# Two of the four sums of weight quarters per feed-forward unit made by accumulating transfers instead of VectorE

## The chip, the cores and the metric

The kernel runs on one core of one Trainium2 chip. The metric is the time that the device takes for one execution, in microseconds (us); comparisons are between medians of several runs.

## What is computed

The reference is two stacks of layers over a sequence of 512 tokens of width 1024. The first stack has two layers, each with a feed-forward block, a mixer (stick-breaking attention beside a gated delta rule), a cross attention to a memory and a second feed-forward block. The second stack has two layers of hybrid attention with a gated residual. All of it is in fp32. The change touches the four feed-forward blocks alone:

```python
def swiglu_ffn(x, w_in, w_out):          # w_in: 1024 x 5632, w_out: 2816 x 1024
    gate, up = jnp.split(x @ w_in, 2, axis=-1)
    return (jax.nn.silu(gate) * up) @ w_out

for l in range(DEPTH):                   # DEPTH = 2
    h = h + 0.5 * swiglu_ffn(rms_norm(h, ffn1_norm[l]), ffn1_w_in[l], ffn1_w_out[l])
    h = h + hybrid_mixer(...)
    h = h + memory_cross_attention(...)
    h = h + 0.5 * swiglu_ffn(rms_norm(h, ffn2_norm[l]), ffn2_w_in[l], ffn2_w_out[l])
```

## The kernel before

TensorE multiplies in a rounded fp32 format. To keep accuracy each operand is split into a rounded part (`hi`, made by ScalarE, line 394) and the rest (`lo`, made by VectorE, line 395), and every product is three matmuls: hi with hi, hi with lo, lo with hi.

A feed-forward block (`ffn`, line 472) has 11 units of 256 hidden columns. Units 0 and 1 are computed plainly (`ffn_plain`). Units 2 to 10 are computed by `ffn_seven_steps` (line 549) with Strassen's scheme in Winograd's form: the input projection of a unit is a 2 x 2 product of blocks, gate and up columns by the two halves of the 1024 inputs, and is made with seven block products instead of eight. The sums of the activations that the scheme needs are made once per block (`seven_parts`, line 522). The sums of the weights are made per unit: with the quarters b11 (gate, first half), b12 (up, first half), b21 (gate, second half) and b22 (up, second half), each 128 x 1024 fp32 or 512 KB, they are p1 = b11 + b12, p2 = p1 + b22, b12 + b22 and p2 + b21. All four are made by VectorE (`tt`, line 562).

The seven products of a unit come in the order b11, p2, b12 + b22, p1, b21, p2 + b21, b22. Ahead of each, `parts` rounds its weights: a ScalarE cast into a tile `sh` and a VectorE subtraction into a tile `sl`, two buffers of each. So the rounding for one product can start when the product two before it has been computed. Below, the "third rounding" of a unit is the pair of cast and `sl` for its third product, and so on. `product` (line 580) issues 24 matmuls of 256 columns. A `yield` behind each product lets `ffn` put one or two steps of the output projection of earlier units between the products (line 274 on TensorE). In unit 2, the first of a block that uses seven products, there are no earlier units whose output projection could run, so its products follow each other directly.

The weight quarters and their sums lie in tiles with the tag `sr`, of which there are six. They are taken in program order and a tile is reused when its last reader is done; a transfer that is to fill one waits for that. In a unit of the kernel before they are taken by b11, b12, p1, b22, p2 and b21.

All weight transfers go through SP's queue in order (`load`, lines 564 to 567 for the quarters; line 266 for the other weights). The code in `with ahead()` is given a priority 110 instructions earlier than its place, so loads, sums and roundings run ahead of the products. The order of the instructions on each engine is made by a scheduler when the program is built; on the chip each engine takes its own in that order and waits on semaphores. POOL (GpSimd) has next to nothing to do in the feed-forward blocks.

Of the kernel before, what the change touches and what calls it, by code (L numbers as in the profile page):

```python
# [14 lines left out]
ALU = mybir.AluOpType  # L15
# [162 lines left out]
class Builder:  # L178
# [370 lines left out]
    def ffn_seven_steps(self, name, l, u, ap, xh, xl, s, R, t, act):  # L549

        nc = self.nc
        toks = slice(0, HS), slice(HS, S)
        A = lambda th, kh: [x[:, 4 * kh : 4 * kh + 4, toks[th]] for x in (xh, xl)]
        ahead = lambda: self.tc.high_priority(offset=FF_AHEAD)
        T = lambda: ap.tile([P, 4, 256], F32, name=self.uid("sr"), tag="sr", bufs=6)
        v = lambda x: x.rearrange("p (j c) -> p j c", j=2)  # L560
        Rh = [R[:, ts].unsqueeze(1).to_broadcast([P, 2, HS]) for ts in toks]
        tt = lambda o, a, b, op=ALU.add: nc.vector.tensor_tensor(out=o, in0=a, in1=b, op=op)

        def load(c, kh):
            w = T()
            nc.sync.dma_start(out=w, in_=self.waps(name + "_in", l, 2 * u + c).rearrange("p (k c) -> p k c", k=8)[:, 4 * kh : 4 * kh + 4])
            return w

        def parts(w):
            x = [ap.tile([P, 4, 256], F32R, name=self.uid(n), tag=n, bufs=2) for n in ("sh", "sl")]  # L570
            self.split(*x, w)
            return x

        def product(ps, w, x, first=True):
            for j in range(2):
                fs = slice(j * P, (j + 1) * P)
                for k in range(4):
                    start = first and j == 0 and k == 0
                    for i, (a, b) in enumerate(((0, 0), (0, 1), (1, 0))):
                        nc.tensor.matmul(ps[:, j], w[a][:, k, fs], x[b][:, k], start=start and i == 0, stop=k == 3 and i == 2, skip_group_check=True)  # L580

        xt = lambda tag: v(self.xp.tile([P, S], F32, name=self.uid(tag), tag=tag, bufs=1))
        a, b, c, d = (self.ps("d", [P, 2, HS]) for _ in range(4))
        with ahead():
            b11 = load(0, 0)
            w = parts(b11)
        product(a, w, A(0, 0))
        m1 = xt("acc")
        nc.scalar.copy(m1, a)
        yield  # L590
        with ahead():
            b12 = load(1, 0)
            p1 = T()
            tt(p1, b11, b12)
            b22 = load(1, 1)
            p2 = T()
            tt(p2, p1, b22)
            w = parts(p2)
        product(b, w, s["s2"])
        V = xt("sq")  # L600
        tt(V, m1, b)
        yield
        with ahead():
            tt(b12, b12, b22)
            w = parts(b12)
        product(c, w, s["s3"])
        x22 = v(t("uu"))
        tt(x22, V, c)
        yield
        with ahead():  # L610
            w = parts(p1)
        product(d, w, s["s1"])
        tt(x22, x22, d)
        tt(x22, x22, Rh[1], ALU.mult)
        yield
        with ahead():
            b21 = load(0, 1)
            w = parts(b21)
        product(a, w, A(0, 1), False)
        gates = v(t("gg")), v(t("gg"))  # L620
        ss = [v(t("ss")) for _ in range(2)]
        tt(gates[0], a, Rh[0], ALU.mult)
        nc.scalar.activation(out=ss[0], in_=gates[0], func=AF.Silu)
        yield
        with ahead():
            tt(p2, p2, b21)
            w = parts(p2)
        product(c, w, A(1, 1), False)
        tt(gates[1], V, c)
        tt(gates[1], gates[1], Rh[1], ALU.mult)  # L630
        nc.scalar.activation(out=ss[1], in_=gates[1], func=AF.Silu)
        yield
        with ahead():
            w = parts(b22)
        product(d, w, s["s4"], False)
        x12 = v(t("uu"))
        tt(x12, V, d)
        tt(x12, x12, Rh[0], ALU.mult)
        for th, x in ((1, x22), (0, x12)):
            nc.vector.scalar_tensor_tensor(out=x, in0=x, scalar=-1.0, in1=ss[th], op0=ALU.mult, op1=ALU.mult)  # L640
            self.split(*(y[:, :, toks[th]] for y in act), x)
        yield
# [1013 lines left out]
```

## Time and profile before

| | us |
|---|---|
| median of 3 runs | 3196.88 |
| lowest and highest run | 3195.92, 3201.14 |
| the profiled execution, its own time | 3195.22 |
| span of the profiled execution, first to last instruction | 3192.9 |
| TensorE busy | 3134.1 |
| VectorE busy | 2326.2 |
| ScalarE busy | 1451.7 |
| POOL busy | 133.8 |

The profile is of one execution. Times in it are counted from the start of its span. Busy times overlap, since the engines work beside each other. TensorE's granted clock is at its full level in the four stretches that the change touches.

### The profile page before, as it was taken

What the parts mean: (1) busy time and instruction counts of PE and PEld (TensorE: products, weight loads), DVE (VectorE), ACT (ScalarE), POOL (GpSimd) and SP (SyncE); (2) the same over time, 40 slices, a digit from 0 to 9 for tenths busy, and PEclk for the clock granted to TensorE, in tenths of its full rate; (3) what the DMA queues carried; (4) which work ended last, traced back from release to release, by engine and by line L of the source; (5) the groups of instructions that cost most, each with busy time, mean ns of one, the idle gap of its engine ahead of it and who ended that gap; (6) DMA issues with size and microseconds to landing.
All of it is one profiled execution on the core that took longest, in us unless ns stands there. A gap on an engine that the chain in (4) does not pass through costs nothing. (4 is left out here: it accounts for less than half of the span.)

```text
span 3192.9 us, 50423 instructions
## 1 busy us (share of the span) xinstructions
PE 3134.1 (98%) x20520; PEld 2718.9 (85%) x20520; DVE 2326.2 (73%) x3952; ACT 1451.7 (45%) x2291; POOL 133.8 (4%) x182
## 2 busy tenths in 40 slices
PE   8999999989999999999999989999999999999999
PEld 7999877778889998999877868889998987799877
DVE  8887567776588877888657686578886667766675
ACT  5344542544443434334452354453343556445563
POOL 0000002220000000000002040000000000000000
PEclk9999999999999999999999999999999999999999
DMA  4332220323233323333221223133332322223223
GB/s 165 97 118 81 87 73 28 95 71 113 67 125 95 107 76 117 100 103 101 70 86 34 82 65 119 60 125 99 101 95 72 100 80 80 76 90 100 72 73 101
DMA packets 86728, 287.32 MB, mean 90 GB/s; under 512 B 10080, under 2 KB 13408, under 8 KB 86496
## 3 DMA queue, kind: packets, MB, share of 16 engines
q1 hardware_dynamic: 86496, 284.10, 28.7%
q8 instruction: 161, 2.64, 0.3%
q14 instruction: 71, 0.58, 0.1%
HBM read 269.38 MB, written 2.10 MB: 85 GB/s over the span
## 5 line engine op out<-in xcount | busy, mean ns | idle before, releaser
L268 DVE TENSOR_TENSOR wl<-wr,wh 128x1024 fp32r<-128x1024 f32 (+3 forms) x384 | 443.1, 1154 | 211.4 <-ACT wh L267 209.4
L267 ACT CAST wh<-wr 128x1024 fp32r<-128x1024 f32 (+3 forms) x384 | 378.1, 985 | 399.4 <-PE psd L274 285.9
L394 ACT CAST sh<-sr 128x1024 fp32r<-128x1024 f32 x252 | 264.8, 1051 | 503.7 <-PE psd L580 474.4
L274 PE MATMUL psd<-xh,wh 128*128 128x512 f32 x960 | 387.0, 403 | 7.2 <-ACT xh L397 7.2
L274 PE MATMUL psd<-xl,wh 128*128 128x512 f32 x960 | 385.5, 402 | 0.2 <-DVE xl L398 0.2
L274 PE MATMUL psd<-xh,wl 128*128 128x512 f32 x960 | 384.9, 401 | 0.2 <-DVE wl L268 0.2
L580 PE MATMUL psd<-xh,sl 128*128 128x256 f32 x1152 | 322.7, 280 | 5.2 <-DVE sl L395 5.2
L580 PE MATMUL psd<-xh,sh 128*128 128x256 f32 x1152 | 322.5, 280 | 0.0
L580 PE MATMUL psd<-xl,sh 128*128 128x256 f32 x1152 | 321.9, 279 | 0.0
L395 DVE TENSOR_TENSOR sl<-sr,sh 128x1024 fp32r<-128x1024 f32 x252 | 307.3, 1220 | 15.1 <-ACT sh L394 14.2
L274 PE MATMUL psd<-wh,xh 128*128 128x256 f32 (+1 forms) x1024 | 292.1, 286 | 1.0 <-ACT wh L267 0.9
L274 PE MATMUL psd<-wh,xl 128*128 128x256 f32 (+1 forms) x1024 | 289.9, 283 | 1.2 <-DVE xl L398 1.1
L274 PE MATMUL psd<-wl,xh 128*128 128x256 f32 (+1 forms) x1024 | 289.0, 283 | 0.0
L274 PE MATMUL psd<-ah,wh 128*128 128x512 f32 x704 | 278.2, 395 | 0.0
L274 PE MATMUL psd<-al,wh 128*128 128x512 f32 x704 | 278.0, 395 | 0.0
L274 PE MATMUL psd<-ah,wl 128*128 128x512 f32 x704 | 277.0, 394 | 0.0
L274 PEld LDWEIGHTS psd<-xh,wh 128*128 128x128 f32 x960 | 181.2, 189 | 53.9 <-ACT xh L397 7.2
L580 PEld LDWEIGHTS psd<-xh,sl 128*128 128x128 f32 x1152 | 216.9, 188 | 6.8 <-DVE sl L395 6.8
L580 PEld LDWEIGHTS psd<-xh,sh 128*128 128x128 f32 x1152 | 216.8, 188 | 5.3
L580 PEld LDWEIGHTS psd<-xl,sh 128*128 128x128 f32 x1152 | 216.8, 188 | 4.8
L274 PEld LDWEIGHTS psd<-xh,wl 128*128 128x128 f32 x960 | 181.5, 189 | 42.1 <-issue 1.2
L274 PEld LDWEIGHTS psd<-xl,wh 128*128 128x128 f32 x960 | 181.5, 189 | 39.9 <-DVE xl L398 1.0
(452 smaller groups left out, 6999.2 us busy)
## 6 DMA issues: line engine op xcount, KB each, us to landing
sr<-w_ffn_in_dram SPq DMA_DIRECT2D x144, 512.0 KB, 3.9
wr<-w_ffn_out_dram SPq DMA_DIRECT2D x96, 384.0 KB, 4.0
wr<-w_ffn_in_dram SPq DMA_DIRECT2D x32, 512.0 KB, 3.8
wr<-w_mix_gdn_dram SPq DMA_DIRECT2D x24, 512.0 KB, 3.7
B<-B SPq DMA_DIRECT2D x40, 256.0 KB, 3.4
wr<-w_ffn_out_dram SPq DMA_DIRECT2D x16, 512.0 KB, 3.4
wr<-w_mix_qk_dram SPq DMA_DIRECT2D x16, 512.0 KB, 3.8
wr<-w_x_k_dram SPq DMA_DIRECT2D x16, 512.0 KB, 3.7
```

Of the source, the lines that this page charges most:

```text
L267: nc.scalar.copy(hi, raw)
L268: (nc.gpsimd if name in ON_POOL else nc.vector).tensor_sub(lo, raw, hi.bitcast(F32))
L274: mm = lambda a, b, first, last: nc.tensor.matmul(ps, a, b, start=first, stop=last, skip_group_check=flip)
L394: nc.scalar.copy(hi, src)
L395: nc.vector.tensor_tensor(out=lo, in0=src, in1=hi.bitcast(F32), op=ALU.subtract)
L580: nc.tensor.matmul(ps[:, j], w[a][:, k, fs], x[b][:, k], start=start and i == 0, stop=k == 3 and i == 2, skip_group_check=True)
```

## The change

A helper `src` names a weight quarter in memory. `load` takes a second quarter, `more`: after the plain transfer on SP's queue a second transfer, issued by POOL, adds that quarter to the same tile while it is written. p1 = b11 + b12 is loaded so (b11 a second time, b12 added), and so is b12 + b22, as b22 a second time with b12 added. The two VectorE sums for these go, and so does the plain load of b12 alone. The `sr` tiles of a unit are then taken by b11, p1, b22, p2, b22 + b12 and b21; b11's tile is no longer read by a sum.

```diff
+        src = lambda c, kh: self.waps(name + "_in", l, 2 * u + c).rearrange("p (k c) -> p k c", k=8)[:, 4 * kh : 4 * kh + 4]
+
-        def load(c, kh):
+        def load(c, kh, more=None):
+
             w = T()
-            nc.sync.dma_start(out=w, in_=self.waps(name + "_in", l, 2 * u + c).rearrange("p (k c) -> p k c", k=8)[:, 4 * kh : 4 * kh + 4])
+            nc.sync.dma_start(out=w, in_=src(c, kh))
+            if more:
+                nc.gpsimd.dma_start(out=w, in_=src(*more), accum_op=ALU.add)
             return w
...
         with ahead():
-            b12 = load(1, 0)
-            p1 = T()
-            tt(p1, b11, b12)
+            p1 = load(0, 0, (1, 0))
             b22 = load(1, 1)
             p2 = T()
             tt(p2, p1, b22)
...
         with ahead():
-            tt(b12, b12, b22)
-            w = parts(b12)
+            w = parts(load(1, 1, (1, 0)))
         product(c, w, s["s3"])
```

## Rows read from the trace of the kernel before

**Rows 1.** The page, busy time of each engine: us, share of the span, instructions.

```profile
PE 3134.1 (98%) x20520; PEld 2718.9 (85%) x20520; DVE 2326.2 (73%) x3952; ACT 1451.7 (45%) x2291; POOL 133.8 (4%) x182
```

**Rows 2.** Stretches with seven-product units: us, busy time by engine (instructions), clock, DMA, GB/s.

```profile
57.40:326.90 269.50, 268.98 (x1905) 251.42 (x1904) 219.89 (x275) 109.53 (x137) 1.25 (x6) 1.00 0.32 100
...
sum 1077.50, PE 1072.32 PEld 1002.47 DVE 867.98 ACT 427.37 POOL 2.51; mean PE 268.08 PEld 250.62 DVE 217.00 ACT 106.84 POOL 0.63
```

**Rows 3.** Waits of TensorE: us in total, times, longest us.

```profile
PE psd L580 <- DVE sl L395: 5.2, 8, 1.8
```

**Rows 4.** Groups by line and shape, VectorE: busy us, mean ns, idle before, releaser.

```profile
L395 DVE TENSOR_TENSOR sl<-sr,sh 128x1024 fp32r<-128x1024 f32 x252 | 307.3, 1220 | 15.1 <-ACT sh L394 14.2
...
L562 DVE TENSOR_TENSOR sr<-sr,sr 128x1024 f32<-128x1024 f32 x144 | 173.4, 1221 | 18.6 <-DMA sr<-w_ffn_in_dram 17.7
```

**Rows 5.** Waits of SP's queue: us in total, times, longest us.

```profile
SPq L566 <- DVE sl L395: 772.8, 120, 8.9
```

**Rows 6.** Stretch from the start to the first seven-product unit, columns as in rows 2.

```profile
0.00:57.40 57.40, 49.77 (x208) 39.46 (x209) 47.25 (x88) 34.21 (x48) 1.53 (x10) 1.00 0.54 182
```

**Rows 7.** DMA issues (KB each, median us to landing) and landing times of `sr` loads.

```profile
sr<-w_ffn_in_dram SPq DMA_DIRECT2D x144, 512.0 KB, 3.9
...
wr<-w_s_ple_dram SPq DMA_DIRECT2D x8, 256.0 KB, 2.6
...
DMA to landing us min/median/max: 3.5/3.9/7.6
```

**Rows 8.** Timeline of a handover beside output steps: start, us, engine, line, what.

```profile
241.73 0.33 SPq L566 DMA_DIRECT2D sr<-w_ffn_in_dram  x1
...
250.06 1.23 DVE L395 TENSOR_TENSOR sl<-sr,sh 128x1024 fp32r<-128x1024 f32 x1 [0.28 <-ACT sh L394]
251.21 0.95 DVE L268 TENSOR_TENSOR wl<-wr,wh 128x768 fp32r<-128x768 f32 x1
252.66 0.69 DVE L562 TENSOR_TENSOR uu<-uu,psd 128x512 f32<-128x512 f32 x1 [0.50 <-PE psd L580]
253.38 0.69 DVE L562 TENSOR_TENSOR uu<-uu,R 128x512 f32<-128x512 f32 x1
253.99 1.22 DVE L395 TENSOR_TENSOR sl<-sr,sh 128x1024 fp32r<-128x1024 f32 x1
255.33 2.36 DVE L562 TENSOR_TENSOR sr<-sr,sr 128x1024 f32<-128x1024 f32 x2
...
258.97 0.28 PE L580 MATMUL psd<-xh,sl 128*128 128x256 f32 x1
...
269.19 1.22 DVE L395 TENSOR_TENSOR sl<-sr,sh 128x1024 fp32r<-128x1024 f32 x1
```

**Rows 9.** Timeline of the first block's first seven-product unit.

```profile
62.62 0.33 SPq L566 DMA_DIRECT2D sr<-w_ffn_in_dram  x1
...
66.44 1.22 DVE L562 TENSOR_TENSOR sr<-sr,sr 128x1024 f32<-128x1024 f32 x1 [0.98 <-DMA sr<-w_ffn_in_dram]
...
69.45 0.39 PE L580 MATMUL psd<-xh,sl 128*128 128x256 f32 x1 [0.21 <-DVE sl L395]
...
70.64 1.22 DVE L395 TENSOR_TENSOR sl<-sr,sh 128x1024 fp32r<-128x1024 f32 x1
...
72.36 0.28 PE L580 MATMUL psd<-xh,sl 128*128 128x256 f32 x1
...
73.21 1.23 DVE L562 TENSOR_TENSOR sr<-sr,sr 128x1024 f32<-128x1024 f32 x1 [0.19 <-DMA sr<-w_ffn_in_dram]
74.36 1.22 DVE L395 TENSOR_TENSOR sl<-sr,sh 128x1024 fp32r<-128x1024 f32 x1
...
75.63 0.39 PE L580 MATMUL psd<-xh,sl 128*128 128x256 f32 x1 [0.30 <-DVE sl L395]
```

**Rows 10.** Timeline of the third block's first seven-product unit.

```profile
1286.02 1.22 DVE L562 TENSOR_TENSOR sr<-sr,sr 128x1024 f32<-128x1024 f32 x1 [0.98 <-DMA sr<-w_ffn_in_dram]
...
1294.33 1.22 DVE L562 TENSOR_TENSOR sr<-sr,sr 128x1024 f32<-128x1024 f32 x1 [1.74 <-DMA sr<-w_ffn_in_dram]
```

## The prediction

> **What bounds the kernel now.** The page's busy times come first: TensorE is busy for 3134.1 of 3192.9 us, VectorE for 2326.2 [rows 1]. The change lies in the four feed-forward blocks, so the next view is the table of stretches over the part of each block in which the seven-product units run (nine units each, 36 in all): of 1077.50 us TensorE is busy for 1072.32, VectorE for 867.98 [rows 2]. The reader is to see two things there. VectorE has about a fifth of its time free; and TensorE stands still for 1077.50 - 1072.32 = 5.2 us in all four stretches together. The view of waits says what for: matmuls of line 580 waited eight times for a `sl` from VectorE, 5.2 us in total, 1.8 at the longest [rows 3]. So whatever VectorE is spared, these stretches can give back 5.2 us at most, 0.16% of the time. VectorE's sums are not on the path that sets the end, but a VectorE that stands waiting can get onto it.
>
> **What the change removes.** Of the 144 sums on line 562, 1.22 us each [rows 4], two per unit go: 72 x 1.22 = 88 us of VectorE. All of it lies beside TensorE's work; on the path it is worth a share of the 5.2 us.
>
> **What it adds.** Per unit one more plain load on SP (five for four) and two accumulating ones issued by POOL, each of which must wait for the plain load that fills its tile. POOL does nothing else in the stretches but a few memsets, so no one queues behind these waits there. On SP the extra issue costs nothing as long as tiles, not SP, set the pace, and they do: 120 loads waited for a `sl`, 772.8 us [rows 5]. The extra traffic is three 512 KB reads per unit, 108 x 0.524 MB = 56.6 MB, in 1077.50 us 53 GB/s on top of about 100 there; the first 57 us moved 182 GB/s [rows 6], so bandwidth covers it.
>
> What counts is the time L from the landing of the plain load to that of the accumulating one, because the sum that VectorE still makes of the two (p2 = p1 + b22) needs it, and VectorE takes its instructions in order. No accumulating transfer is in the trace. A plain 512 KB load lands after a median of 3.9 us, a 256 KB one after 2.6 [rows 7]: that is about 1.3 us fixed and 2.6 per 512 KB. An addition to what is already there has to move the new and the old data: 1.3 + 2 x 2.6, my estimate is **L = 6.4 us**. The lower end is a plain load's 3.9; the upper, three such loads one after another (read, read back, write), 11.7. A gain below 3.9 has no reason, since the source is the same. The Trainium skill, page "DMA: Bandwidth & Descriptors", section on the anatomy of a DMA from GpSimd, gives 2.0 us plus bytes over 436 GB/s for one issued there, 3.2 us for this size by an estimate from it; it is for a plain copy, and no run here shows one from that queue. By it nothing in the sum below would be late, and the first rival's time would hold.
>
> **Where L is covered: a unit beside output steps.** 28 of the 32 handovers between units are of this kind. The six `sr` tiles go round in the order in which they come free. The plain half of p1 takes the tile that the third rounding pair has read, so its load starts where one starts today, at 241.73, and lands 3.9 later at 245.63; with L it is summed at 252.0. p2 takes the tile of b21, free when the fifth `sl` ends (250.06 + 1.22 = 251.28), one rounding earlier than today's 255.33 [rows 8], where all times of this part stand. VectorE waits 0.7 us there in the worst order. Behind the sum stand a `wl`, two evictions and the sixth `sl`: 1.23 + 0.95 + 0.69 + 0.69 + 1.22 = 4.78, which ends at 256.8, and the matmul that reads that `sl` runs at 258.97. Cost nothing, with 2.2 us left. The other new tile, s = b22 + b12, takes the tile freed by the sixth `sl` (255.21): 255.21 + 3.9 + 6.4 = 265.5, and its `sl` is at 269.19, behind its ScalarE cast: covered too, and its VectorE sum is gone from ahead of it.
>
> **Where it is not: the first unit of each block, four times.** There nothing runs between the products, and all eight TensorE waits stand here, two in each block [rows 9]. Today p1's sum for the next unit waits for its load and holds up the fifth `sl`; the p2 sum then stands right ahead of the seventh `sl` [rows 9]. In the changed kernel p1's sum is no longer in VectorE's queue, so the fifth `sl` is on time. The load is issued at 62.62 and had landed by 66.44; with L, 72.84. That is before 73.21, where p2's sum stands now, so if p2's sum stays ahead of the seventh `sl`, that `sl` comes about 0.3 us earlier, in three of the four blocks alike. In the third block p2's sum waited 1.74 us for b22, whose load the new order starts a rounding earlier: 1286.02 + 6.4 = 1292.4 against 1294.33 [rows 10], 1.9 us earlier. **Sum:** 3 x 0.3 + 1.9 = 2.8 us less. The profiled execution took 3195.22, so 3192.4; the median of the three runs is 1.66 above it, so **3194**. This is a change of 0.1%, below the 0.2% that a measurement here can tell from none.
>
> **Rivals.** *All waits go.* If the accumulation takes no longer than a plain load, 3.9, all 5.2 us vanish: 3191.7. For it: VectorE loses 88 us and has no late input left. Against it: the seventh `sl` also follows a p2 sum and a rounding cast, which stay.
>
> *The sum moves ahead.* p2's tile comes free at the fifth `sl`, so the scheduler may put its sum ahead of the sixth `sl` in the first unit, where it stands behind it today. VectorE then waits until 72.84, and sum and `sl` end 2 x 1.22 later, at 75.28; the matmul that needs this `sl` was at 72.36 [rows 9], 72.0 without the wait that is gone. That is 3.3 us in each of four blocks, 13.2 - 5.2 = 8.0 more: 3204.9, slower by 0.25%. For it: p1's sum stands right behind the `sl` that freed its tile today. Against it: an order by when data come would put the sixth `sl` first.
>
> *The accumulation is long.* In units beside output steps the path is touched once 241.73 + 3.9 + L + 4.78 passes 258.97, that is from **L = 8.6** on; each microsecond more then costs up to 28 us, for VectorE waits in order and everything behind p2's sum is late. At 11.7 it is 3.1 x 28 = 87 there and 4 x 5.3 - 2.8 = 18 in the first units, some 3302. For it: plain loads already took up to 7.6 us to land [rows 7], and these come on top of more traffic. What could stretch them is POOL, which has to issue them, held up by a VectorE that is busy four fifths of the time. The Trainium skill, page "SBUF — State Buffer", box on VectorE blocking a DMA, says that a transfer issued from GpSimd starves while VectorE runs a copy in a two-port mode, 620 ns becoming 3100. By that, L would grow by 2.5 us to 8.9 and the time by some 16 us. The same page says that a tensor_tensor has no such mode, and the VectorE groups of rows 4 are all tensor_tensor; so the trace gives this rule little hold here.
>
> **How the numbers follow.** The forecast (L from about 4 to 8, p2's sum behind the sixth `sl`) has 0.55, all waits gone 0.16, the sum ahead 0.14, long accumulations 0.15. Faster by over 0.2% means below 3190.5, which even the whole 5.2 us does not reach; it takes that and a lucky order elsewhere, or scatter: 0.07 from the first rival, 0.03 from the forecast. Slower by over 0.2% means above 3203.3: 0.15 from long accumulations, 0.12 from the sum ahead. The rest, 0.63, is no difference. The range goes from 3190 (3191.7 less the 1.0 by which the lowest run lay under the median, rounded out) to 3220: the sum ahead lies within it, and so do long accumulations up to L = 9.0, where (9.0 - 8.6) x 28 + 4 x 2.6 - 2.8 = 19 us are added to 3196.9, and the highest run lay 4 above the median. Only longer accumulations are left out above.
>
> **What would show it.** Right: VectorE's busy time lower by some 88 us, 72 sums left on line 562, TensorE's idle time in the four stretches still a few us, with waits for `sl` in the first units alone. L is read from the accumulating transfers' landing times. The sum ahead shows as one wait of some 3 us per block before a sixth product; long accumulations as `sr` sums on VectorE waiting for DMA by several us in most units, and TensorE waiting for `sl` in them. The prediction is wrong if TensorE's idle time grows in units beside output steps, if ScalarE's cast of s waits for its transfer, or if time moves outside these four stretches, of which the sum says nothing.

## The result and the profile after

| | before | after |
|---|---|---|
| median, us | 3197.95 (4 runs, 3195.92 to 3201.14) | 3227.98 (4 runs, 3225.65 to 3232.56) |
| span of the profiled execution, us | 3192.9 | 3224.8 |
| ratio, 95% interval | | 1.0096, 1.0084 to 1.0109 |

The changed kernel is slower by 0.96%. That is outside the predicted range, which ended at 3220.

First the page of the changed kernel: busy time by engine, the two DMA queues (packets, MB, share of 16 engines' span), and the issues of `sr` tiles.

```profile
PE 3141.7 (97%) x20520; PEld 2726.4 (85%) x20520; DVE 2238.0 (69%) x3880; ACT 1452.2 (45%) x2291; POOL 196.2 (6%) x254
...
q1 hardware_dynamic: 91680, 302.97, 30.6%
q0 software_dynamic: 10368, 37.75, 6.6%
...
sr<-w_ffn_in_dram SPq DMA_DIRECT2D x180, 512.0 KB, 4.5
...
sr<-w_ffn_in_dram POOLq DMA_DIRECT2D x72, 512.0 KB, 7.6
```

The change does what it says: VectorE is busy for 88.2 us less than in [rows 1]. The accumulating transfers take a median of 7.6 us from issue to landing, and the plain ones have gone from 3.9 [rows 7] to 4.5. TensorE is busy for longer, 3141.7 against 3134.1, with the same 20520 matmuls.

The table of the four stretches (columns as in [rows 2]), its first row and the sum:

```profile
57.17:340.97 283.80, 273.87 (x1905) 255.95 (x1904) 200.31 (x259) 109.22 (x136) 14.90 (x22) 0.98 0.52 138
...
sum 1107.14, PE 1082.41 PEld 1012.48 DVE 788.59 ACT 427.00 POOL 57.63; mean PE 270.60 PEld 253.12 DVE 197.15 ACT 106.75 POOL 14.41
```

Of the 31.9 us that the span grew by, 1107.14 - 1077.50 = 29.6 lie here. TensorE's idle time has gone from 5.2 to 1107.14 - 1082.41 = 24.7, that is 19.5 more; the other 10.1 are busy time, the same matmuls at a lower clock. The waits of TensorE (us in total, times, longest) name the places:

```profile
PE psd L585 <- DVE sl L395: 19.2, 5, 5.4
PE psd L274 <- ACT xh L397: 8.3, 1, 8.3
PE psn L428 <- DVE acc L419: 5.5, 1, 5.5
...
PE psn L405 <- DVE rc L388: 2.7, 2, 1.4
```

The second row lies ahead of the first block's units and was 7.2 us before; the others are new or longer.

**The first unit of each block** (here and below, the first that uses seven products). Measured from the first matmul of a unit to that of the next, these took 26.6, 27.4, 26.0 and 26.6 us against 20.9, 22.4, 22.5 and 21.0: 19.8 more. The timeline of the one in the first block (it answers to [rows 9]):

```profile
66.59 0.85 POOL L571 DMA_DIRECT2D sr<-w_ffn_in_dram  x1 [27.31 <-DMA sr<-w_ffn_in_dram]
...
73.84 1.23 DVE L562 TENSOR_TENSOR sr<-sr,sr 128x1024 f32<-128x1024 f32 x1 [4.35 <-DMA sr<-w_ffn_in_dram]
74.98 1.22 DVE L395 TENSOR_TENSOR sl<-sr,sh 128x1024 fp32r<-128x1024 f32 x1
...
76.26 0.58 PE L585 MATMUL psd<-xh,sl 128*128 128x256 f32 x1 [4.42 <-DVE sl L395]
```

The sum on VectorE is p2's. It stands ahead of the sixth `sl` and holds VectorE for 4.35 us until the accumulation has landed; TensorE then stands for that `sl`. The matmul at 76.26 takes 0.58 us, twice the usual 0.28. The windows of the same stretch say why:

```profile
72.00:74.00 2.00, 0.00 (x0) 0.00 (x0) 0.16 (x1) 0.56 (x1) 0.00 (x0) 0.98 0.22 43
74.00:76.00 2.00, 0.00 (x0) 0.00 (x0) 2.00 (x2) 0.00 (x0) 0.00 (x0) 0.50 0.00 0
76.00:80.00 4.00, 3.74 (x17) 3.75 (x18) 2.53 (x4) 0.63 (x1) 0.00 (x0) 0.50 0.46 154
80.00:84.00 4.00, 4.00 (x33) 4.00 (x32) 2.80 (x4) 1.78 (x3) 0.86 (x1) 0.90 0.61 136
```

TensorE did nothing between 72 and 76, the granted clock fell from 1.00 to 0.50 (1.2 of 2.4 GHz) and stayed there until past 80, so the products behind the wait ran at half speed for over 4 us. The Trainium skill, page "TensorE: Matmul & The Clock Gate", Part 1, says that the low clock is the default and that activity lifts it; the rows agree.

**Unit 6 of the first block**, 41.3 us against 32.6. Here the memory of the cross attention is read in eight 128 KB loads (`memT`), squared by ScalarE and summed by VectorE, and matmuls of line 428 sum the result. From the timeline, with the rows of SP, POOL, ScalarE and TensorE:

```profile
187.82 0.33 SPq L569 DMA_DIRECT2D sr<-w_ffn_in_dram  x1
...
188.72 0.85 POOL L571 DMA_DIRECT2D sr<-w_ffn_in_dram  x1 [15.10 <-DMA sr<-w_ffn_in_dram]
...
189.00 7.93 SPq L1099 DMA_DIRECT2D memT<-memT_dram  x3
...
196.16 0.42 ACT L418 ACTIVATE sq<-memT 128x256 f32<-128x256 f32 x1 [3.79 <-DMA memT<-memT_dram]
...
200.90 0.80 PE L428 MATMUL psn<-consts,acc 128*128 128x1 f32 x3 [5.50 <-DVE acc L419]
```

A small load issued at 189.0, right behind a plain 512 KB load and an accumulating one, was read only at 196.16. The landing times of these eight loads in the changed kernel, and below them in the kernel before:

```profile
DMA to landing us min/median/max: 2.4/3.1/7.1
```

```profile
DMA to landing us min/median/max: 2.4/2.4/2.9
```

TensorE stood for 5.5 us and then ran at half clock, as the window behind it shows:

```profile
201.00:206.00 5.00, 5.00 (x20) 4.61 (x21) 3.87 (x13) 1.43 (x2) 0.86 (x1) 0.50 0.32 105
```

**The heads of the second and third block** lost 1.4 us each. In the second, p2's sum for the first seven-product unit stands within a chain of small VectorE steps (lines 386 to 388) at whose end TensorE waits:

```profile
914.32 1.23 DVE L562 TENSOR_TENSOR sr<-sr,sr 128x1024 f32<-128x1024 f32 x1 [1.41 <-DMA sr<-w_ffn_in_dram]
...
917.10 0.15 DVE L388 SCALAR_TENSOR_TENSOR rc<-rs_t,rs_y 128x4 f32<-128x4 f32 x1
```

19.8 + 8.7 + 2.7 is 31.2 of the 31.9 us. What is left are differences of both signs between two executions.

### The profile page after: what moved, and what is told of

Read it like the earlier page. It is cut to its first block, busy times and chain, and to the rows that moved or that the text cites. A ratio compares the mean times of both kernels' runs of the same rounds, so it can differ in the third digit from the quotient of the medians.

```text
span 3224.8 us, 50695 instructions
## 1 busy us (share of the span) xinstructions
PE 3141.7 (97%) x20520; PEld 2726.4 (85%) x20520; DVE 2238.0 (69%) x3880; ACT 1452.2 (45%) x2291; POOL 196.2 (6%) x254
## 3 DMA queue, kind: packets, MB, share of 16 engines
q0 software_dynamic: 10368, 37.75, 6.6%
```

## The experiments

The kernel before ran beside each group of runs (medians 3195.76 to 3196.82). "First units" is the sum of the four lengths as above, "unit 6" that of the first block; both are read from the one profiled execution of each kernel, in us. Each median is of 4 to 11 executions, that of e8 of two.

| kernel | us | ratio, 95% interval | first units | unit 6 |
|---|---|---|---|---|
| before | 3196 | | 86.8 | 32.6 |
| changed | 3227.98 | 1.0084 to 1.0109 | 106.6 | 41.3 |
| e1 copy instead of add | 3209.84 | 1.0027 to 1.0057 | 92.6 | 38.0 |
| e2 p2's sum behind the sixth `sl` | 3217.77 | 1.0051 to 1.0081 | 99.3 | 41.3 |
| e3 memory's sums later | 3225.71 | 1.0071 to 1.0105 | 107.6 | 39.1 |
| e4 both | 3213.07 | 1.0035 to 1.0065 | 91.6 | 38.3 |
| e5 no second transfer | 3191.91 | 0.9982 to 1.0001 | 81.2 | 33.6 |
| e6 units 6, 7 as before | 3220.27 | 1.0062 to 1.0095 | 106.0 | 32.6 |
| e7 exposed units as before | 3199.05 | 0.9998 to 1.0017 | 85.1 | 32.6 |
| e8 second transfer twice | 3553.77 | 1.1101 to 1.1145 | 85.4 | 49.7 |
| e9 p1's tile first | 3212.00 | 1.0038 to 1.0063 | 85.6 | 40.1 |
| e10 e9, units 6, 7 as before | 3203.14 | 1.0013 to 1.0032 | 85.7 | 32.8 |
| e11 b22 + b12 alone | 3196.62 | 0.9994 to 1.0012 | 81.7 | 34.6 |
| e12 p1 alone | 3226.93 | 1.0082 to 1.0109 | 99.4 | 38.7 |
| e13 e10, first units' own sums as before | 3198.90 | 0.9995 to 1.0013 | 85.3 | 32.6 |
| e14 e11, units 6, 7 as before | 3192.78 | 0.9979 to 0.9997 | 81.7 | 32.6 |

Theory at the start: the loss is VectorE standing for p1's accumulation in the first units, because the sum of p2 has moved ahead, plus the memory's late loads. Rival: the transfers cost something everywhere, by their traffic.

**e1, a copy in the place of the addition.**

```diff
-                nc.gpsimd.dma_start(out=w, in_=src(*more), accum_op=ALU.add)
+                nc.gpsimd.dma_start(out=w, in_=src(*more))
```

> The changed kernel, but the second transfer of each pair copies instead of adding; so the two sums lack their first summand (this part of the computation is left out). Same queues, same traffic, same order of VectorE's instructions. Theory: the addition itself makes the transfer long (7.6 us median from issue to landing, against 4.5 for the plain one on SP), and both losses come from that. Then the landing falls to about 4 to 4.5 us, VectorE's p2 sum in the first unit starts at about 66.6 + 4.4 = 71.0 instead of 73.84, the sixth `sl` ends 2.9 us earlier, the wait of TensorE there shrinks from 4.4 to about 1.6 us and is too short for the clock to fall; the memory's loads land in 3 us and the wait of 5.5 us in the seventh unit goes. Time: 3228 less 4 x 4 less 8.7 = 3203 (3199 to 3208). Rival: it is the traffic or POOL's queue, whatever the transfer does; then the landing stays at 7 us or more and the time at 3224 to 3232.

The page's row of POOL's queue:

```profile
q0 software_dynamic: 10368, 37.75, 3.3%
```

The landing times of its transfers:

```profile
DMA to landing us min/median/max: 3.8/5.0/6.5
```

VectorE's p2 sum in the first unit, from the timeline:

```profile
71.51 1.22 DVE L562 TENSOR_TENSOR sr<-sr,sr 128x1024 f32<-128x1024 f32 x1 [2.20 <-DMA sr<-w_ffn_in_dram]
```

The same bytes take half the engine time (3.3% for 6.6%) and land in 5.0 for 7.6 us. Of the first units' 19.8 us 14 go, and 18 of the 31 us altogether. The waits of TensorE there were 1.9 to 2.4 us, not 1.6, and it still waited 3.5 us for the memory's sums: a copy on POOL landed later than a load on SP (5.0 against 3.9 in the same execution), and the memory's loads still came late beside it. The expectation also took the wait to be too short for the clock to fall; it fell behind two of the four waits (units of 24.0 us each) and not behind the others (22.1 and 22.5). So the addition makes up the larger part, the second transfer by itself the rest. The time lies just over the 3199 to 3208 expected.

**e2, the order alone; e3, the memory's sums later; e4, both.**

```diff
             b22 = load(1, 1)
+            s12 = load(1, 1, (1, 0)) if u == FF_PLAIN + 1 else None
             p2 = T()
...
-            w = parts(load(1, 1, (1, 0)))
+            w = parts(s12 or load(1, 1, (1, 0)))
```

> The changed kernel, but in the second seven-product unit of each block the tile for b22 + b12 is taken ahead of the one for p2, so that p2's tile comes free only at the sixth `sl` of the first unit and its sum stands behind that `sl`. Nothing else. Theory (the sum moves ahead): the place of this sum in VectorE's queue is what costs the first units 5.7, 5.0, 3.5 and 5.6 us; then these go, TensorE's one long wait per block with them, and the time is 3228 - 20 = 3208 (3204 to 3212); the wait for the memory's sums in the first block stays. Rival (the transfers themselves take something from the first units, by bandwidth or late loads): another wait for `sl` comes in its place, and the time stays above 3220.

VectorE in the first unit of e2:

```profile
70.04 1.22 DVE L395 TENSOR_TENSOR sl<-sr,sh 128x1024 fp32r<-128x1024 f32 x1
73.75 1.23 DVE L562 TENSOR_TENSOR sr<-sr,sr 128x1024 f32<-128x1024 f32 x1 [2.49 <-issue]
...
75.49 1.22 DVE L395 TENSOR_TENSOR sl<-sr,sh 128x1024 fp32r<-128x1024 f32 x1
```

The sixth `sl` is on time, but the sum starts when it did, at 73.75 (the row names no releaser; p1's accumulation landed at 73.7), and now the seventh `sl` is late: TensorE waited 2.2 us there (5.2 in the second block). In the execution profiled (3222.80 us, the four of e2 going from 3211.97 to that) the order is worth 7.3 of the 19.8 us, not all of them. Both sides missed: the median fell between them.

The edit of e3 keeps the squares' sum in a lasting tile and calls the rest later:

```diff
-        rc = self.stats(tiles(), width=MEM)
+        nc.vector.tensor_copy(self.mem_r, self.squares(tiles(), None, MEM))
...
+        self.mean_rsqrt(self.token_sums(self.mem_r), rc)
```

> The changed kernel, but the two matmuls that sum the squares of the memory over its width, with what follows from them, come three units later; the loads and squares stay where they are (the squares' sum is copied to a tile that lasts). Theory: 8.7 us of the loss are this one wait of TensorE (5.5 us, for the last of eight 128 KB loads) and the half clock behind it; then 3228 - 8.7 = 3219 (3216 to 3222), and the first units stay as they are. Rival: the late loads also hold up ScalarE, which stands for them ahead of the casts of the weights; then a wait for `sl` or `wl` takes the place of this one in the same unit and less than 4 us come back: 3224 or more.

The waits of TensorE in e3 have a new row in the place of line 428's:

```profile
PE psd L590 <- ACT acc L599: 3.6, 1, 3.6
```

The rival held: ScalarE, which stands for the late loads, evicts a product too late, and unit 6 got back only 2.2 us.

> Both edits at once: the sum of p2 behind the sixth `sl` in the first units, and the memory's sums three units later. Theory: the two losses are independent and together the whole: 3228 - 20 - 8.7 = 3199 (3194 to 3203), no difference from the kernel before that could be measured, with 88 us less of VectorE. Rival: something else in the change costs time over all units (traffic, 72 longer transfers): then 3206 or more.

3213: the two give back 14.9 us together, about what they gave one by one (10.2 and 2.3), and the expectation failed with them. The time lies in the rival's range, but e7 below speaks against a cost over all units. The first units have the same edit as in e2 and yet lost only 4.8 us in the execution profiled (3207.30 us, the four of e4 going from that to 3217.14). TensorE's waits in them were much the same (2.2 us in three blocks, 3.0 in the second), but only the one in the second block was followed by half clock; in e2 all four were. The first block, behind its wait of 2.2 us, in e2 and below it in e4:

```profile
78.00:80.00 2.00, 2.00 (x11) 2.00 (x11) 1.77 (x3) 0.63 (x1) 0.00 (x0) 0.50 0.80 127
```

```profile
78.00:80.00 2.00, 2.00 (x20) 2.00 (x19) 1.83 (x3) 1.10 (x2) 0.00 (x0) 1.00 0.84 143
```

So the order is worth 7 to 15 us, by whether the clock falls behind a wait of this length. That this is also what sets the executions of one kernel some us apart is likely, but not shown.

**e5, the second transfer left out.** This measures what VectorE's 88 us are worth.

```diff
             nc.sync.dma_start(out=w, in_=src(c, kh))
-            if more:
-                nc.gpsimd.dma_start(out=w, in_=src(*more), accum_op=ALU.add)
```

> The changed kernel without the second transfer of each pair: p1 is b11 alone, and b22 + b12 is b22 alone (the two additions are left out). VectorE has the same 3704 instructions, with the p2 sum ahead of the sixth `sl` in the first units. Theory of the prediction: VectorE's 88 us lie beside TensorE's work, so even when nothing has to be waited for in their place at most the 5.2 us of waits can go: 3196.4 less 0 to 5.2, that is 3191 to 3197. Rival: VectorE's busy time is on the path in more places than the waits show; then 3185 or less. If instead the plain loads' order alone delays the memory's loads, the wait of the seventh unit in the first block stays and the time is 3200 or more.

The busy times on its page, and below them the sum of the four stretches:

```profile
PE 3134.4 (98%) x20520; PEld 2718.9 (85%) x20520; DVE 2240.7 (70%) x3880; ACT 1451.3 (45%) x2291; POOL 133.8 (4%) x182
```

```profile
sum 1073.43, PE 1072.23 PEld 1002.74 DVE 791.08 ACT 425.90 POOL 2.51; mean PE 268.06 PEld 250.68 DVE 197.77 ACT 106.47 POOL 0.63
```

85.5 us less of VectorE bring 4.2 us, and the interval just reaches no difference; 1.2 of the 5.2 us of idle time are left. (The page counts 3880 instructions of VectorE, as for the changed kernel, not the 3704 of the expectation.) The ceiling that the prediction drew was right. The p2 sum stands ahead of the sixth `sl` here too: that order costs nothing as long as its data are there.

**e6, units 6 and 7 of the first block as before; e7, also the second seven-product unit of each block** (whose p2 sum is the one made during the first).

```diff
-            p1 = load(0, 0, (1, 0))
+            if u == FF_PLAIN + 1 or (l, name, u) in ((0, "ffn1", 6), (0, "ffn1", 7)):
+                b12 = load(1, 0)
+                p1 = T()
+                tt(p1, b11, b12)
+            else:
+                p1 = load(0, 0, (1, 0))
```

(and b22 + b12 likewise; e6 without the first condition)

> The changed kernel, but units 6 and 7 of the first block, beside which the memory is read in eight 128 KB loads, make their sums on VectorE as before; the other 34 units accumulate. Theory: a small load issued right behind a plain 512 KB load and an accumulating one lands only when both have (7.1 us against at most 2.9), ScalarE stands for it, and TensorE with it. Then in this unit nothing is late any more, and the 8.7 us come back: 3228 - 8.7 = 3219 (3215 to 3222), with the memory's loads landing in 3 us again. Rival: the memory's loads are late by the order on SP's queue, which the change shifts from the start of the block on; then the wait stays: 3225 or more.

> The changed kernel, but where nothing covers the accumulation (the second seven-product unit of each block, and units 6 and 7 of the first block) the sums are made on VectorE as before. Accumulating transfers stay in 30 of the 36 units. Theory: in the other handovers they cost nothing and bring nothing; all of the 30 us come back: 3196.4 (3193 to 3200), with VectorE 73 us less busy. Rival: the transfers cost a little in every unit, or elsewhere by traffic: 3203 or more.

The landing times of the memory's loads in e6:

```profile
DMA to landing us min/median/max: 2.3/2.4/2.7
```

Both came out as the theory said: 7.7 us back in e6, and in e7, with accumulation still in 30 units, 29 of the 30 us. What is left in e7, 3 us within its interval of no difference, has its largest part in the heads of blocks as above, where TensorE waited 2.9 us.

**e8, the second transfer twice**, as a test of the prediction's threshold L = 8.6.

```diff
             if more:
-                nc.gpsimd.dma_start(out=w, in_=src(*more), accum_op=ALU.add)
+                for _ in range(2):
+                    nc.gpsimd.dma_start(out=w, in_=src(*more), accum_op=ALU.add)
```

> The changed kernel with the accumulating transfer issued twice in each pair, one after the other (so the second quarter is added twice, and the result is another). L, from the landing of the plain load to the end, goes from about 7.8 to about 15.5. The prediction said that beside output steps each microsecond over L = 8.6 costs up to 28 us in all. In the changed kernel the sixth `sl` there still ends 0.7 to 2.7 us ahead of its matmul, so a delay of 7.7 us leaves some 6 in each of the 28: 28 x 6 = 168, and 4 x 6 in the first units: 3228 + 190 = 3420 (3340 to 3460). Rival: the order of VectorE's instructions, made with the longer transfers in view, puts the p2 sum later and covers most of it: below 3300.

Waits of TensorE, and below them the busy times on the page:

```profile
PE psd L586 <- DVE sl L395: 223.2, 53, 10.7
...
PE psn L405 <- DVE rc L388: 20.7, 3, 9.0
PE psd L586 <- ACT sh L394: 15.6, 12, 2.3
PE psn L428 <- DVE acc L419: 11.5, 1, 11.5
```

```profile
PE 3226.8 (91%) x20520; PEld 2794.0 (79%) x20520; DVE 2236.2 (63%) x3880; ACT 1450.9 (41%) x2291; POOL 257.8 (7%) x326
```

The waits for `sl` grew by 204 us, near the 192 worked out (6 us at 32 handovers): beyond the threshold nearly every microsecond is paid at each handover. One part went as the rival said, without helping: in the first units the p2 sum now stands behind the seventh `sl`, so these took 85.4 us together, and its wait of 8.1 to 8.4 us falls on the unit after. But the time grew by 326. The sum had left out TensorE's clock (3226.8 - 3141.7 = 85 us more busy time) and the waits in the other three rows (18 + 16 + 6 more).

**e9 to e14: which sum, and does any form help?** In e9 p1 takes its tile ahead of b11, so that its accumulation starts two roundings earlier.

```diff
         with ahead():
+            p1 = load(0, 0, (1, 0))
             b11 = load(0, 0)
...
-            p1 = load(0, 0, (1, 0))
             b22 = load(1, 1)
```

> The changed kernel, but each unit takes p1's tile ahead of b11's, so that p1's plain half starts where b11's did: two roundings earlier, 2 x 2.88 = 5.8 us in the first units. The accumulation that landed at 73.8 in the first block then lands at about 68, before the fifth `sl` ends (68.9), although VectorE's order still has the p2 sum ahead of the sixth `sl`. Theory: not the order and not the accumulation by themselves, but the time between the start of the accumulation and the sum that needs it, is what costs; then the first units go down to the 20.3 us that they take without the second transfer, the waits at the head of the second and third block go too, and only the memory's loads may still be late: 3192 to 3201. Rival: the transfers slow something by their traffic wherever they stand: 3205 or more.

> The same, and units 6 and 7 of the first block make their sums on VectorE, so that the memory's loads stand beside no accumulating transfer. Theory: nothing of the loss is left, and the waits of TensorE for `sl` in the four stretches go as in the run without second transfers: 3192 (3189 to 3197), at best 0.15% faster than the kernel before. Rival: each of the 34 units pays something that shows in no wait: 3200 or more.

The first units fell to 85.6 us, with the same order on VectorE; what is left of waiting in them, 1.1 to 1.4 us each, hangs on b22's load, issued later now. So it is the time between the start of the accumulation and its reader that costs. The 3212 of e9 are above what was expected: unit 6 stayed at 40.1, the four units behind the first ones took 2.6 us more, and an accumulation that went ahead of the start's own loads cost 4.7 us before the first unit (it began at 62.1, and in e13, which has no accumulation there, at 57.5). e10 had 3203, its nine runs from 3196.31 to 3209.72: by its time that is the rival's range, though e7 with 30 units accumulating came to 3199. Its profiled execution was one of the shortest, 3196.72, so that no trace shows where the longer ones lost time, and the cause stays open.

> Only b22 + b12 is accumulated; p1 = b11 + b12 stays on VectorE, with b12 loaded for it. Theory: the loss hangs on p1, because VectorE stands for it in order, and because the transfer beside the memory's loads is p1's; b22 + b12 is read by ScalarE's cast, with time to spare. Then 3196 (3193 to 3200), VectorE 44 us less busy. Rival: each accumulated sum carries its half of the loss: 3208 to 3216.

> Only p1 is accumulated; b22 + b12 stays on VectorE. In VectorE's order the p2 sum then stands behind the sixth `sl` in the first block's first unit, as the prediction's forecast had it. Theory: p1 carries the loss, and L is about 7.5 instead of the predicted 6.4, so that in this order too the p2 sum and with it the seventh `sl` are late, by about 2.4 us per block, as in the run that changed the order alone; the memory's wait stays: 3196.4 + 4 x 2.4 - 2 + 8.7 = 3213 (3207 to 3221). Rival (the order was all): 3205 or less.

```diff
+            b12 = load(1, 0)
-            w = parts(load(1, 1, (1, 0)))
+            tt(b12, b12, b22)
+            w = parts(b12)
```

(that is e12; e11 keeps the accumulation of b22 + b12 and makes p1 by `tt`)

By the medians p1 alone carries the whole loss, b22 + b12 nothing. It does not stand in the same places, though: in e12 12.6 us lie in the first units, 6.1 in unit 6, and some 7 ahead of the second and third block, where TensorE waited 4.8 us for line 388 (2.7 in the changed kernel). In e12 the p2 sum stands where the prediction's forecast had it, behind the sixth `sl`; VectorE in the first unit:

```profile
70.86 1.22 DVE L395 TENSOR_TENSOR sl<-sr,sh 128x1024 fp32r<-128x1024 f32 x1
...
76.22 1.22 DVE L562 TENSOR_TENSOR sr<-sr,sr 128x1024 f32<-128x1024 f32 x1 [4.14 <-DMA sr<-w_ffn_in_dram]
77.96 1.21 DVE L395 TENSOR_TENSOR sl<-sr,sh 128x1024 fp32r<-128x1024 f32 x1
```

The sum waited for 4.14 us in that order too, more than in e2. What it waited for is another transfer: p1's accumulation, issued at 67.41, landed at 74.98, and the plain load of b22, issued on SP's queue at 68.86, landed after it, at 76.09. The view of this load, who waited for it and its landing time:

```profile
  DVE sr L562: 4.1, 1
...
DMA to landing us min/median/max: 7.2/7.2/7.2
```

In the kernel before, b22's load at 69.42 took 3.7 us. In the other three blocks of e12, too, it was this load that landed last, 6.5 to 6.9 us after its issue. So the expectation had the place of the wait, and a cause that was only part of it; the time is above the 3207 to 3221 expected.

> As the run with p1's tile first and units 6 and 7 on VectorE, and also the first seven-product unit of every block makes its sums on VectorE. So no accumulation stands in the first 57 us, nor ahead of the chain of small VectorE steps at the head of a block; 30 units accumulate. Theory: the run before this one lost 4.4 us in the first 57 us to an accumulation that was put ahead of the start's own loads, and the rest of its loss (its median lay 7 above its profiled execution) to accumulations at places where VectorE or a load's landing decides; then 3193 (3190 to 3197). Rival: the scatter has to do with the transfers themselves: median 3200 or more again, with executions 10 us apart.

> Only b22 + b12 is accumulated, and not in units 6 and 7 of the first block; 34 accumulating transfers. Theory: the two waits that were left in the run with b22 + b12 alone (1.6 us for the memory's sums, 1.9 us for `sl`) shrink by the first one: 3194 (3190 to 3198), which can't be told from the kernel before. Rival: nothing of it was due to the accumulating transfer beside the memory's loads: 3196.5 or more.

e13 adds the condition `u == FF_PLAIN` to those under which e10 sums on VectorE. Its median of 3198.9 lies between the theory and the rival, its executions 8 us apart, and what is left isn't settled. e14 is e11 with units 6 and 7 as before. It is the one form that came out faster than the kernel before, by 0.12% (0.03 to 0.21): VectorE 41 us less busy, no accumulation that VectorE stands for, none beside the memory's loads. It is one of several forms tried, and the gain is close to what scatter can make.

## Why the prediction was wrong, step by step

**Held.** VectorE's 88 us lie beside TensorE's work; at most 5.2 us can come back (e5: 4.2). p1's sum is gone from ahead of the fifth `sl`, and no fifth product waited. The wait of p2's sum was the place to look at, in the first units above all. Of the 28 handovers beside output steps 27 cost nothing, with little to spare; the one in the first block that answers to [rows 8]:

```profile
267.75 1.22 DVE L562 TENSOR_TENSOR sr<-sr,sr 128x1024 f32<-128x1024 f32 x1 [1.48 <-issue]
...
269.49 1.22 DVE L395 TENSOR_TENSOR sl<-sr,sh 128x1024 fp32r<-128x1024 f32 x1
...
273.08 0.28 PE L585 MATMUL psd<-xh,sl 128*128 128x256 f32 x1
```

The `sl` ends at 270.71, 2.4 us ahead of its matmul. Over the others this rest went down to 0.7 us; in one, late in the fourth block, the `sl` came too late and the unit took 0.5 us more. ScalarE's cast of b22 + b12 was covered, as said (e11). POOL was not held up by VectorE: a median of 0.56 us passed between a plain landing and the accumulation's issue, at most 1.23, so that rival had no hold.

**L was sized too small.** The prediction put 6.4 us: 1.3 fixed, and 2.6 each for the new and the old data. In the first unit p1's plain half was issued at 62.50 and landed 3.5 us later, at 66.0; the accumulation was issued at 66.59 and landed 7.2 later, at 73.8, and it was needed by 73.21. That is L = 7.7 there, 7.0 to 7.9 in the four first units, and a median of 8.2 (7.0 to 9.1) over p1's 36. The addition's own part was right: 7.6 less 5.0 for a copy on the same queue (e1) is 2.6. What failed is what it was added to, a plain load of the trace of before: a copy on POOL takes 5.0 and not 3.9, and the 0.56 us from the plain landing to POOL's issue were put at nothing; 5.0 + 2.6 + 0.56 = 8.2. The Trainium skill's page "DMA: Bandwidth & Descriptors", section on the anatomy of a DMA from GpSimd, gave 3.2 for a copy; the measurements decide, 5.0 for the copy and 7.6 with the addition.

**So the forecast's case could not hold, in either order.** With p2's sum behind the sixth `sl` the prediction expected 2.8 us of gain; e2 and e12 have that order and lose 12.5 and 12.6 us in the first units. In e2 the sum waits for the accumulation, in e12 for b22's plain load beside it, which the prediction left at the landing time of before. The rival *the sum moves ahead* (0.14) is what the changed kernel shows, and what the two rivals had as separate cases, order and L, was one case: e1 and e2 each give back part of it.

**The price of that rival was under half of the true one.** It had 13.2 - 5.2 = 8.0 us; measured were 19.8. The waits were 4.3 to 5.4 us rather than 3.3, since L was longer, 19.0 in place of 13.2; and the term of the clock was missing: all four of these waits, and the one for the memory's sums, were followed by stretches at half clock, together 10.1 us of added busy time.

**Two places were not looked at.** The sum covered the loads that the change adds, and not the loads of others that queue behind them: the memory's 128 KB loads, 8.7 us (e6). And it left out a block's head, where the p2 sum of the first unit stands in a chain that TensorE waits for, 2.7 us. The prediction said that it would be wrong if time moved to where its sum said nothing; this is that.

## What to carry to other kernels

Here 88 us of work moved from an engine with room to transfers could buy 4.2 us at most, and a transfer's latency has to be covered at every place where an engine that works in order stands for it: look for the places without cover first (the first turn of a loop, its head, a short chain of other work). Add to each wait of TensorE the stretch at half clock that may follow it, and list the transfers, the small ones above all, that will stand behind the new ones. Choose for such a transfer an operand whose reader has time to spare, as e14 does.

## What the runs showed of the hardware

- An accumulating transfer took twice the DMA engines' time of a copy of the same 37.75 MB (6.6% against 3.3% of 16 engines' span), and 7.6 against 5.0 us to land. Its issue held POOL for 0.85 us against 0.53 for the copy (at 66.59 in the changed kernel, at 66.52 in e1).
- A 128 KB load issued behind 1 MB on its way landed after 7.1 us instead of 2.4 to 2.9, although it was on SP's queue and the accumulation on POOL's. A plain 512 KB load issued 1.45 us behind an accumulation took 7.2 us instead of 3.7 (e12, at 68.86).
- After TensorE had stood from 71.8 to 76.3 its granted clock was 0.50, and the first matmul took 0.58 instead of 0.28 us. Such stretches cost 10 us in the changed kernel and 85 more in e8. Behind a wait of 2.2 us the clock fell to 0.50 in e2 and stayed at 1.00 in e4.
